# Routed experts with few tokens: two weight passes in place of three, chosen by a branch on TensorE

## The chip, the cores and the metric

One core of a Trainium2 chip runs the whole program in one launch. The metric is the device time of an execution in microseconds (us); less is better. Engines are named as the profile names them: PE (TensorE matmul), PEld (TensorE weight load), DVE (VectorE), ACT (ScalarE), POOL (GpSimd), SP (SyncE, which issues the weight loads).

## What is computed

Two decoder layers over 256 tokens of width 1024: each has a modulated RMSNorm, a mixer of two attention groups, and a feed-forward part (dense in layer 0, experts in layer 1). The change is in the experts of layer 1. Everything is float32.

```python
def moe_swiglu(h, router_w, w_gate, w_up, w_down):
    t = h.reshape(B * S, D)                                   # 256 x 1024
    top_v, top_i = lax.top_k(t @ router_w, 2)
    top_w = jax.nn.softmax(top_v, axis=-1)
    gates = sum of one_hot(top_i, 8) * top_w
    for e in range(8):                                        # w_gate, w_up 1024 x 3584, w_down 3584 x 1024
        y = y + gates[:, e:e + 1] * swiglu(t, w_gate[e], w_up[e], w_down[e])
```

swiglu is (silu(h @ w_gate) * (h @ w_up)) @ w_down. Computing the reference's router on its own inputs gives the tokens of the eight experts: 68, 62, 71, 84, 60, 28, 77 and 62. Experts 1, 4, 5 and 7 have at most 64.

## The kernel before

A float32 product is made of rounded halves: an operand x becomes hi (x in the matmul's float32r format) and lo (x - hi), and a product is the three matmuls hi*hi, hi*lo and lo*hi. So every weight, loaded by SP in units of 128x2048 (1 MiB, tile `raw`, 8 buffers), passes through ACT (`whi`, L160) and DVE (`wlo`, L181). The class `Stream` (`ws`) hands them out in the order of use; it converts as far ahead as its 4 places for `whi` and 3 for `wlo` are free, and SP loads a new unit when DVE is done with an old one.

In `experts` the router picks two experts per token. `pick` makes a 0/1 matrix that gives each token of an expert one of CAP = 128 slots (`pk`; its transposes `back` put results back), `gather` multiplies it with the tokens' hi and lo parts, and ACT copies that to `xe`, for two experts at a time. A branch (`overflow`, L1201) handles experts of more than 128 tokens; here it is passed by.

Then 8 experts x 7 chunks of 512 hidden columns follow. A chunk uses six weight units: two for gate and two for up (`wide`, L1028: 8 values of k, three matmuls of 512 columns each), two for down (`down`, L1071: 4 values of f, six matmuls each). The stationary operand is the 128 slots, hi or lo; the weights move. The order within a chunk is written out by hand: gate of chunk c; in it, after k = 5, `turn` transposes the product of chunk c-1 (L1054) and ACT and DVE split it to `g_hi` (L444) and `g_lo` (L445); silu of gate on ACT (L1149); up of c; down of c-1; and in that, behind f = 1, the product silu * up on DVE (L1167). `finish` (L1084 to L1100: gate row, split, scatter matmul, add to `x_sb`) of an expert is spread over the first two chunks of the next one; `pick` and `gather` of the next two experts stand in the last chunks of experts 1, 3 and 5.

Of the kernel before, what the change touches and what calls it, by code (L numbers as in the profile page):

```python
# [14 lines left out]
F32 = mybir.dt.float32  # L15
# [8 lines left out]
P = 128  # L24
# [9 lines left out]
E = 8  # L34
# [6 lines left out]
FOX_SCALE = 0.125  # L41
NEG = -1.0e30
CAP = P


V_ADAB, V_ATTN, V_FFN, V_QN, V_KVN, V_OUT, V_FB = 0, 48, 56, 64, 66, 67, 75
# [193 lines left out]
def trunk_kernel(ctx: ExitStack, tc: tile.TileContext, x, c, positions, w_early, w_moe, router_w,  # L240
# [656 lines left out]
    def experts(l, outer, ps_x, rs):  # L897
# [8 lines left out]
        posm = outer.tile([P, NB, E], F32, name="posm")  # L906
        gates = outer.tile([P, NB, E], F32, name="gates")
        most = outer.tile([P, 1], I32, name="most")
        w = outer.tile([P, 4, NB], F32, name="w")
        oh = outer.tile([P, 2, NB, E], F32, name="oh")  # L910
        gap(outer, 416)

        def shift_col(k):
            return mod[l][:, 24 + k:25 + k]

        back, xe = {}, {}

        def pick(e):

            pk = outer.tile([P, NB, 2, CAP], F32R, name="pick")  # L920
            for j in range(2):
                for b in range(NB):
                    nc.vector.tensor_scalar(pk[:, b, j], iota, posm[:, b, e + j:e + j + 1], None, ALU.is_equal)
            yield pk
            for j in range(2):
                ps = bank("B", [P, S], "ps_b")
                for b in range(NB):
                    nc.tensor.transpose(ps[:, b * P:(b + 1) * P], pk[:, b, j].bitcast(F32), ident)  # L928
                bt = outer.tile([P, S], F32R if e + j + 1 < E else F32, tag="back", name="back", bufs=3)
                nc.scalar.activation(bt, ps, AF.Copy)  # L930
                back[e + j] = bt
            yield pk

        with tc.tile_pool(name="route", bufs=1, reuse_waits="tile") as pool:
# [48 lines left out]

            nc.vector.scalar_tensor_tensor(posm, ps_p[:, 0:2], 1.0, sel, ALU.add, ALU.mult)
            nc.vector.tensor_scalar(posm, posm, -1.0, None, ALU.add)
            picked = pick(0)
            pk = next(picked)

            def gating():
# [7 lines left out]
                                            w[:, 2 + j, :, None].to_broadcast([P, NB, E]), ALU.mult)  # L997
                nc.vector.tensor_add(gates, of[:, 0], of[:, 1])

            overflow(l, hT, posm, gating, gates, most, [put.args[-1] for put in puts])  # L1000
            ws.pump(1, lazy=True)
            ws.rest(2)

        with tc.tile_pool(name="moe", bufs=1, reuse_waits="tile") as pool:
            def gather(e, pk):

                xe[e], xe[e + 1] = [], []
                for k0 in range(0, KD, 2):
                    for k in range(k0, k0 + 2):
                        both = pool.tile([P, 2, 2, CAP], F32R, name=f"xe{k}")  # L1010
                        ps = bank("B", [P, 2, 2, CAP], "ps_g")
                        for i, part in enumerate((h_hi, h_lo)):
# [3 lines left out]
                        nc.scalar.activation(both, ps, AF.Copy)  # L1016
                        for j in range(2):
                            xe[e + j].append((both[:, 0, j], both[:, 1, j]))
                    yield

            def wide(e, ps):
                for k in range(KD):
                    xe_hi, xe_lo = xe[e][k]
                    c = halves[k % 2]
                    if k % 2 == 0:
                        hi, lo = ws.half()
                    for lh, w in ((xe_hi, hi), (xe_hi, lo), (xe_lo, hi)):
                        nc.tensor.matmul(ps, lh, w[:, c], start=(k == 0 and lh is xe_hi and w is hi),  # L1028
                                         stop=(k == KD - 1 and lh is xe_lo))
                    yield k  # L1030

            y_ps, jobs = {}, deque()

# [6 lines left out]
            def turn(pend):  # L1040
# [2 lines left out]
                yield e, ch, g  # L1043
                if (e, ch) == (E - 1, CH - 1):

                    spare = [pool.tile([P, 2, 2, CAP], F32R, name=f"xe{f}") for f in range(0, NFC, 2)]
                    groups = [(2 * i, 2 * i + 2, [t[:, 0], t[:, 1]]) for i, t in enumerate(spare)]
                else:
                    groups = [(0, NFC, [pool.tile([P, NFC, CAP], F32R, name=f"g_{w}") for w in ("hi", "lo")])]
                for f0, f1, (hi, lo) in groups:  # L1050
                    n = f1 - f0
                    ps = bank("B", [P, n, P], "ps_gt")
                    for i in range(n):
                        nc.tensor.transpose(ps[:, i], act[:, (f0 + i) * P:(f0 + i + 1) * P], ident)  # L1054
                    split(hi[:, :n], lo[:, :n], ps)
                    g += [(hi[:, i], lo[:, i]) for i in range(n)]
                    yield

            def down(pend):
                e, ch, g = pend  # L1060
                if ch == 0:
                    y_ps[e] = [bank("C", [P, 512], "ps_y") for _ in range(2)]
                for f in range(NFC):
                    hi, lo = ws.half()
                    g_hi, g_lo = g[f]
                    last = ch == CH - 1 and f == NFC - 1
                    steps = [(hf, lh, w) for lh, w in ((g_hi, hi), (g_hi, lo), (g_lo, hi)) for hf in range(2)]
                    if last:
                        steps.sort(key=lambda s: s[0])
                    for hf, lh, w in steps:  # L1070
                        nc.tensor.matmul(y_ps[e][hf], lh, w[:, hf * 512:(hf + 1) * 512],  # L1071
                                         start=(ch == 0 and f == 0 and lh is g_hi and w is hi),
                                         stop=(last and lh is g_lo))
                    yield f
                    step()

# [56 lines left out]
            ahead = gather(0, pk)  # L1133
            next(ahead)
            next(ahead)
            next(picked)
            jobs += [None, None, None, None] + puts + [gating]
            for e in range(E):
                for ch in range(CH):
                    pg = bank("A", [P, FC], "ps_gate")  # L1140
                    for k in wide(e, pg):
# [11 lines left out]
                    if (e, ch) == (E - 1, CH - 1):  # L1153
                        nc.scalar.preload_act_table_set("natural_log_exp_and_others")  # L1154
# [337 lines left out]
```

## Time and profile before

| | before |
|---|---|
| median of 3 runs (lowest, highest) | 1524.0 us (1523.59, 1524.49) |
| the profiled execution: its time, span of its instructions | 1524.38 us, 1522.2 us |
| PE busy, PEld busy | 1491.9 us (98%), 1277.0 us (84%) |
| DVE busy, ACT busy | 1265.4 us (83%), 1004.9 us (66%) |
| DMA | 481.73 MB, mean 316 GB/s |
| granted TensorE clock, mean | 0.995 |

Busy time is the union of an engine's instructions. PE is pipelined: a matmul's recorded 0.39 us overlaps the next one's, so the time that one costs is the distance of two starts. The experts run from about 538 us to the end.

### The profile page before, as it was taken

The page shows a single profiled execution, that of the slowest core. Times are in us where ns is not written, and L with a number is a line of the kernel's source. Part 1 is how long each engine was busy: PE and PEld are TensorE (multiplying, and loading weights), DVE is VectorE, ACT ScalarE, POOL GpSimd, SP SyncE. Part 2 cuts the span into 40 slices and gives each one's busy share as a digit, 9 for nine tenths or more (in the row PEclk, how much of TensorE's full clock was granted, in tenths as well). Part 3 has the DMA queues.
Part 4 walks back from the last instruction along what each step waited for, and adds up shares of the span by engine and source line. Part 5 has one row for each costly group of instructions (what it writes and reads, how often), then busy time and mean ns, then how long its engine had stood idle before and what let it go on. Part 6 is the DMA issues. An engine that isn't in the chain of part 4 may idle for free.

```text
span 1522.2 us, 20572 instructions
## 1 busy us (share of the span) xinstructions
PE 1491.9 (98%) x7985; PEld 1277.0 (84%) x7985; DVE 1265.4 (83%) x1209; ACT 1004.9 (66%) x1068; POOL 12.6 (1%) x20
## 2 busy tenths in 40 slices
PE   8999999999999899999999999999999999999997
PEld 7988999999898678888888888888888888888885
DVE  5988877777776678899889889879889888988987
ACT  5575544444657576777677777677777777776774
POOL 1000000000000000000000000000000000000000
PEclk9999999999999999999999999999999999999999
DMA  9974778778581269999999999999999998999992
GB/s 373 412 268 166 290 276 309 287 291 299 186 291 56 84 257 363 378 364 371 366 347 348 373 367 366 371 340 347 377 370 368 373 362 324 369 372 377 360 370 91
DMA packets 68472, 481.73 MB, mean 316 GB/s; under 512 B 7953, under 2 KB 8593, under 8 KB 10770
## 3 DMA queue, kind: packets, MB, share of 16 engines
q1 hardware_dynamic: 68178, 480.33, 83.1%
q8 instruction: 63, 1.03, 0.3%
q14 instruction: 39, 0.32, 0.1%
q0 software_dynamic: 192, 0.05, 0.0%
HBM read 479.25 MB, written 1.05 MB: 316 GB/s over the span
## 4 chain that ended last, share of the span: by engine, by line
PE 63%; DVE 1%; ACT 0%; issue 0%; DVEq 0%; ACTq 0%
PE ps_y L1071 20%; PE ps_gate L1028 20%; PE ps_up L1028 19%; PE ps_gt L1054 2%; PE ps_g L1014 1%; DVE wlo L181 0%; PE ps_sc L1097 0%; PE ps_sc L1098 0%; ACT whi L160 0%; PE ps_sc L1121 0%; PE ps_b L928 0%; DVE fin L1129 0%; ACT L1154 0%; DVE gate L347 0%; ACT junk L399 0%
## 5 line engine op out<-in xcount | busy, mean ns | idle before, releaser
L181 DVE TENSOR_TENSOR wlo<-raw,whi 128x2048 fp32r<-128x2048 f32 (+1 forms) x474 | 923.8, 1975 | 62.5 <-ACT whi L160 57.2
L160 ACT ACTIVATE whi<-raw 128x2048 fp32r<-128x2048 f32 (+1 forms) x474 | 769.9, 1662 | 158.6 <-PE ps_gu L394 77.4
L1028 PE MATMUL ps_gate<-whi,xe 128*128 128x512 f32 x896 | 301.8, 396 | 0.0
L1028 PE MATMUL ps_up<-whi,xe 128*128 128x512 f32 x896 | 288.3, 390 | 0.0
L1028 PEld LDWEIGHTS ps_up<-whi,xe 128*128 128x128 f32 x896 | 168.3, 188 | 35.3
L1028 PEld LDWEIGHTS ps_gate<-whi,xe 128*128 128x128 f32 x896 | 168.3, 188 | 33.4
L1028 PE MATMUL ps_gate<-wlo,xe 128*128 128x512 f32 x448 | 175.1, 391 | 0.7 <-DVE wlo L181 0.7
L1028 PE MATMUL ps_up<-wlo,xe 128*128 128x512 f32 x448 | 174.9, 390 | 0.1
L1071 PE MATMUL ps_y<-wlo,g_hi 128*128 128x512 f32 x440 | 136.8, 389 | 0.4 <-DVE wlo L181 0.4
L1071 PE MATMUL ps_y<-whi,g_hi 128*128 128x512 f32 x440 | 136.7, 389 | 0.0
L1071 PE MATMUL ps_y<-whi,g_lo 128*128 128x512 f32 x440 | 136.6, 389 | 0.0
L393 PE MATMUL ps_gu<-dT_hi,whi 128*128 128x256 f32 x432 | 122.5, 284 | 0.0
L395 PE MATMUL ps_gu<-dT_hi,wlo 128*128 128x256 f32 x432 | 122.2, 283 | 0.0
L394 PE MATMUL ps_gu<-dT_lo,whi 128*128 128x256 f32 x432 | 122.2, 283 | 0.0
L444 ACT ACTIVATE g_hi<-ps_gt 128x512 fp32r<-128x512 f32 x55 | 33.0, 599 | 127.1 <-PE ps_gt L1054 127.1
L1028 PEld LDWEIGHTS ps_up<-wlo,xe 128*128 128x128 f32 x448 | 84.1, 188 | 19.0 <-DVE wlo L181 1.4
L1028 PEld LDWEIGHTS ps_gate<-wlo,xe 128*128 128x128 f32 x448 | 84.3, 188 | 17.0 <-DVE wlo L181 1.3
L1071 PEld LDWEIGHTS ps_y<-wlo,g_hi 128*128 128x128 f32 x440 | 82.4, 188 | 18.0 <-DVE wlo L181 1.0
L445 DVE TENSOR_TENSOR g_lo<-ps_gt,g_hi 128x512 fp32r<-128x512 f32 x55 | 37.9, 689 | 71.4 <-ACT g_hi L444 71.4
L1071 PEld LDWEIGHTS ps_y<-whi,g_lo 128*128 128x128 f32 x440 | 82.6, 188 | 17.2
L1071 PEld LDWEIGHTS ps_y<-whi,g_hi 128*128 128x128 f32 x440 | 82.3, 188 | 16.9
L393 PEld LDWEIGHTS ps_gu<-dT_hi,whi 128*128 128x128 f32 x432 | 82.8, 192 | 1.2 <-issue 0.2
(295 smaller groups left out, 1926.4 us busy)
## 6 DMA issues: line engine op xcount, KB each, us to landing
raw<-in_w_moe_dram SPq DMA_DIRECT2D x336, 1024.0 KB, 6.9
raw<-in_w_early_dram SPq DMA_DIRECT2D x114, 1024.0 KB, 6.8
raw<-in_w_early_dram SPq DMA_DIRECT2D x6, 512.0 KB, 8.6
gate<-in_ada_b_dram SPq DMA_DIRECT2D x4, 512.0 KB, 5.6
x_sb<-in_x_dram SPq DMA_DIRECT2D x1, 1024.0 KB, 7.3
out_dram<-fin SPq DMA_DIRECT2D x4, 256.0 KB, 2.0
fg<-in_final_g_dram SPq DMA_DIRECT2D x1, 512.0 KB, 4.9
cn<-in_consts_dram SPq DMA_DIRECT2D x1, 192.0 KB, 12.6
```

Of the source, the lines that this page charges most:

```text
L160: self.nc.scalar.activation(hi, raw, AF.Copy)
L181: self.nc.vector.tensor_sub(parts[1], raw, parts[0].bitcast(F32))
L393: nc.tensor.matmul(out_, lh, rh, start=start, stop=False)
L394: nc.tensor.matmul(out_, lh, rl, start=False, stop=False)
L395: nc.tensor.matmul(out_, ll, rh, start=False, stop=stop)
L444: nc.scalar.activation(hi, src, AF.Copy)
L445: nc.vector.tensor_sub(lo, src, hi.bitcast(F32))
L1014: nc.tensor.matmul(ps[:, i], part[:, b, k * P:(k + 1) * P], pk[:, b], start=(b == 0), stop=(b == NB - 1))
L1028: nc.tensor.matmul(ps, lh, w[:, c], start=(k == 0 and lh is xe_hi and w is hi), stop=(k == KD - 1 and lh is xe_lo))
L1054: nc.tensor.transpose(ps[:, i], act[:, (f0 + i) * P:(f0 + i + 1) * P], ident)
L1071: nc.tensor.matmul(y_ps[e][hf], lh, w[:, hf * 512:(hf + 1) * 512], start=(ch == 0 and f == 0 and lh is g_hi and w is hi), stop=(last and l ...
```

## The change

The router also computes, per expert, `stretch` (2 where the expert has at most 64 tokens, else 1), and packs a bit per expert into one integer, `bits`, which PE loads into a register once (L1209). `slotm` = position x stretch spreads a small expert's tokens over the even slots. `xe` and `g` now lie as [hi slots, lo slots] in one row, so that `even` (every second element of the 256) is a stationary operand with 64 hi and 64 lo tokens. On PE each half unit (`by_width`, L941) becomes a branch with two bodies: the wide one has the three passes of before, the narrow one two (`even` with hi, `even` with lo), after which rows 0 to 63 and 64 to 127 of the PSUM tile hold two parts of one sum. `folded` adds them for gate and up: ACT copies the tile to `fold`, and in the narrow body one matmul with `onto` adds its lower half to the upper. The copy is made for every expert. For down, the scatter matrix `back` has both rows of a token, so the scatter sums them. silu now stands behind k = 4 of up, the branch of `product` (L1246) is its own where the chunk before belongs to another expert. POOL makes the rows of `back` (four instructions of 128 columns per expert). In `close` of layer 1 one `wlo` is no longer made ahead of the router, and one conversion ahead of the gather is gone.

A diff cut to the core (dots mark what is left out):

```diff
-            rs.append(row_r(ss, D, "x", ws.rest if b else None))
+            rs.append(row_r(ss, D, "x", ws.rest if b and ws.size == SPLIT else None))
...
+        def by_width(e, wide, narrow, *more):
+            with tc.If((held[0] & (1 << e)) == 0) as cmp:
+                wide()
+            with cmp.Else():
+                for steps in (*more, narrow):
+                    steps()
...
+            nc.vector.tensor_scalar(stretch, ps_p[:, 2], NARROW + 0.5, 1.0, ALU.is_lt, ALU.add)
+            nc.vector.tensor_tensor(slotm, posm, stretch[:, None, :].to_broadcast([P, NB, E]), ALU.mult)
...
+            nc.vector.tensor_copy(bits, sums[:, 0:1])
             overflow(l, hT, posm, gating, gates, most, [put.args[-1] for put in puts])
-            ws.pump(1, lazy=True)
...
-            def wide(e, ps):
+            def wide(e, ps, *sums):
                 for k in range(KD):
-                    xe_hi, xe_lo = xe[e][k]
-                    c = halves[k % 2]
                     if k % 2 == 0:
                         hi, lo = ws.half()
-                    for lh, w in ((xe_hi, hi), (xe_hi, lo), (xe_lo, hi)):
-                        nc.tensor.matmul(ps, lh, w[:, c], ...
+                        def products(*passes):
+                            n = 0
+                            for kk in range(k, k + 2):
+                                both = xe[e][kk]
+                                for part, w in passes:
+                                    n += 1
+                                    nc.tensor.matmul(ps, both[:, part], w[:, halves[kk % 2]], ...
+                        first, second, even = slice(0, CAP), slice(CAP, 2 * CAP), slice(0, 2 * CAP, 2)
+                        by_width(e, partial(products, (first, hi), (first, lo), (second, hi)),
+                                 partial(products, (even, hi), (even, lo)), *(sums if k == 4 else ()))
                     yield k
+            def folded(ps):
+                t = pool.tile([P, FC], F32R, name="fold")
+                nc.scalar.activation(t, ps, AF.Copy)
+                return partial(nc.tensor.matmul, ps, onto, t, start=False, stop=True, skip_group_check=True)
...
+                    by_width(e, partial(turns, ident), partial(turns, spread))
...
+                    by_width(e, partial(products, (first, hi), (first, lo), (second, hi)),
+                             partial(products, (even, hi), (even, lo)), *(sums if f == 1 else ()))
...
+            held.append(nc.tensor.value_load(bits[0:1, 0:1], min_val=0, max_val=(1 << E) - 1))
...
+                    add = folded(pg)
                     act = pool.tile([P, FC], F32, name="act")
-                    nc.scalar.activation(act, pg, AF.Silu)
...
-                    for k in wide(e, pu):
+                    for k in wide(e, pu, add):
+                        if k == 4:
+                            nc.scalar.activation(act, pg, AF.Silu)
...
+                    add = folded(pu)
+                    within = pend is not None and pend[0] == e and (e, ch) != (E - 1, CH - 1)
                     def product():
                         if parts:
+                            if not within:
+                                with tc.If((held[0] & (1 << e)) != 0):
+                                    add()
                             c = parts.popleft()
                             nc.vector.tensor_mul(act[:, c], act[:, c], pu[:, c])
...
-                    for f in down(pend) if pend is not None else ():
+                    for f in down(pend, *((add,) if within else ())) if pend is not None else ():
```

How the instructions of two engines stand. First PE, half a unit of up (k = 4 and 5 of one chunk); of before:

```order
L1028 MATMUL ps_up<-whi,xe_6552 128x512
L1028 MATMUL ps_up<-wlo_5012,xe_6552 128x512
L1028 MATMUL ps_up<-whi,xe_6552 128x512
L1028 MATMUL ps_up<-whi,xe_6559 128x512
L1028 MATMUL ps_up<-wlo_5012,xe_6559 128x512
L1028 MATMUL ps_up<-whi,xe_6559 128x512
```

and of the change, where the rows behind the first UNCONDITIONAL_BRANCH are the narrow body:

```order
L941 COMPARE_AND_BRANCH
L1081 MATMUL ps_up<-whi,xe_6607 128x512
L1081 MATMUL ps_up<-wlo,xe_6607 128x512
L1081 MATMUL ps_up<-whi,xe_6607 128x512
L1081 MATMUL ps_up<-whi,xe_6614 128x512
L1081 MATMUL ps_up<-wlo,xe_6614 128x512
L1081 MATMUL ps_up<-whi,xe_6614 128x512
L941 UNCONDITIONAL_BRANCH
L945 MATMUL ps_gate<-fold,onto 128x512
L1081 MATMUL ps_up<-whi,xe_6607 128x512
L1081 MATMUL ps_up<-wlo,xe_6607 128x512
L1081 MATMUL ps_up<-whi,xe_6614 128x512
```

The six matmuls are now one of two bodies behind a compare and a jump, and the narrow body begins with the sum of the gate's two halves. There are 13 such branches in a chunk: four in gate, four in up, one around the transposes, four in down.

Second ACT, one chunk from the split of the turned product on; of before:

```order
L444 ACTIVATE g_hi<-ps_gt 128x512
L1149 ACTIVATE act<-ps_gate 128x512
L160 ACTIVATE whi_5010<-raw_6778 128x2048
L160 ACTIVATE whi_5011<-raw_6806 128x2048
L160 ACTIVATE whi<-raw_6822 128x2048
L160 ACTIVATE whi<-raw_6838 128x2048
L160 ACTIVATE whi_5010<-raw_6855 128x2048
L160 ACTIVATE whi_5011<-raw_6872 128x2048
L444 ACTIVATE g_hi<-ps_gt 128x512
```

and of the change:

```order
L446 ACTIVATE g<-ps_gt 128x4x128
L941 UNCONDITIONAL_BRANCH x3
L1093 ACTIVATE fold<-ps_gate 128x512
L162 ACTIVATE whi_5010<-raw_7001 128x2048
L941 UNCONDITIONAL_BRANCH
L162 ACTIVATE whi_5011<-raw_7050 128x2048
L941 UNCONDITIONAL_BRANCH
L1231 ACTIVATE act<-ps_gate 128x512
L941 UNCONDITIONAL_BRANCH
L1093 ACTIVATE fold<-ps_up 128x512
L162 ACTIVATE whi<-raw_7080 128x2048
L941 UNCONDITIONAL_BRANCH
```

ACT has two more copies in a chunk (`fold`), the silu (`act`) has moved behind two conversions, and each branch of PE is a jump to the next instruction here.

## Rows read from the trace of the kernel before

**Rows 1.** Page, part 1: busy us, share of the span and instructions of each engine.

```profile
PE 1491.9 (98%) x7985; PEld 1277.0 (84%) x7985; DVE 1265.4 (83%) x1209; ACT 1004.9 (66%) x1068; POOL 12.6 (1%) x20
```

**Rows 2.** Chain of waits, 600 to 1500 us: share by line; one long piece.

```profile
by line: PE ps_gate L1028 31.7%; PE ps_y L1071 31.3%; PE ps_up L1028 31.0%; PE ps_gt L1054 2.5%; PE ps_g L1014 1.3%; PE ps_sc L1097 0.7%; PE ps_sc L1098 0.7%; DVE wlo L181 0.3%; ACT whi L160 0.2%; PE ps_b L928 0.1%; ACT L1154 0.1%; issue 0.
...
659.51 5.46 PE ps_up L1028 x24
```

**Rows 3.** Windows: us; busy us (count) PE, PEld, DVE, ACT, POOL; PEclk; DMA share; GB/s.

```profile
701.91:718.70 16.79, 16.79 (x78) 13.89 (x76) 14.59 (x10) 12.26 (x9) 0.00 (x0) 1.00 0.96 375
790.66:809.00 18.34, 18.34 (x84) 15.15 (x83) 17.64 (x15) 14.32 (x11) 0.00 (x0) 1.00 0.87 343
666.39:790.66 124.27, 124.23 (x578) 103.03 (x577) 108.06 (x69) 91.22 (x69) 0.00 (x0) 1.00 0.94 357
790.66:910.20 119.54, 119.54 (x542) 98.87 (x541) 107.12 (x66) 86.92 (x59) 0.00 (x0) 1.00 0.96 367
```

**Rows 4.** Timeline, DVE: start us, us, line, op, tiles, [idle before <- releaser].

```profile
701.91 0.68 DVE L1167 TENSOR_TENSOR act<-act,ps_up 128x512 f32<-128x512 f32 x1
702.50 6.69 DVE L181 TENSOR_TENSOR wlo<-raw,whi 128x2048 fp32r<-128x2048 f32 x3
711.09 0.69 DVE L445 TENSOR_TENSOR g_lo<-ps_gt,g_hi 128x512 fp32r<-128x512 f32 x1 [1.89 <-ACT g_hi L444]
711.70 2.28 DVE L181 TENSOR_TENSOR wlo<-raw,whi 128x2048 fp32r<-128x2048 f32 x1
714.29 4.50 DVE L181 TENSOR_TENSOR wlo<-raw,whi 128x2048 fp32r<-128x2048 f32 x2 [0.31 <-ACT whi L160]
718.70 0.68 DVE L1167 TENSOR_TENSOR act<-act,ps_up 128x512 f32<-128x512 f32 x1
```

**Rows 5.** Waits, 700 to 736 us (two chunks): us in total, times, longest us.

```profile
ACT g_hi L444 <- PE ps_gt L1054: 5.2, 2, 2.6
DVE g_lo L445 <- ACT g_hi L444: 3.8, 2, 1.9
DVE wlo L181 <- ACT whi L160: 0.6, 2, 0.3
```

**Rows 6.** Waits of SyncE's DMA queue, 600 to 1500 us.

```profile
SPq L142 <- DVE wlo L181: 760.5, 306, 5.2
```

**Rows 7.** Windows, for DMA share and GB/s.

```profile
10.00:65.00 55.00, 52.32 (x413) 51.27 (x413) 42.39 (x69) 31.19 (x59) 1.69 (x3) 0.97 1.02 424
565.00:575.00 10.00, 10.00 (x48) 8.29 (x47) 8.10 (x6) 5.97 (x4) 0.00 (x0) 1.00 1.00 415
600.00:700.00 100.00, 100.00 (x454) 82.72 (x453) 89.78 (x55) 71.90 (x50) 0.00 (x0) 1.00 0.97 370
```

**Rows 8.** Waits, 757 to 777 us, where the next two experts are gathered.

```profile
DVE wlo L181 <- ACT whi L160: 6.1, 4, 2.4
```

**Rows 9.** Timeline, PE, before and behind the overflow branch (L1201), and a gather.

```profile
528.56 0.17 PE L977 MATMUL ps_p<-sel,tri 128*128 128x8 bf16 x1
528.58 0.17 PE L978 MATMUL ps_p<-sel,ones 128*128 128x8 bf16 x1
...
533.67 0.77 PE L1014 MATMUL ps_g<-pick,h_hi 128*128 128x256 f32 x2 [4.85 <-ACT whi L160]
...
540.04 0.40 PE L1014 MATMUL ps_g<-pick,h_hi 128*128 128x256 f32 x2
540.28 0.41 PE L1014 MATMUL ps_g<-pick,h_lo 128*128 128x256 f32 x2
```

**Rows 10.** Timeline, ACT, two conversions with the overflow branch between them.

```profile
529.61 3.94 ACT L160 ACTIVATE whi<-raw 128x2048 fp32r<-128x2048 f32 x2
```

**Rows 11.** Timeline, PEld: a weight load behind idle time with no wait.

```profile
527.03 0.19 PEld L351 LDWEIGHTS ps_fold<-acc,cn 128*128 128x128 f32 x1 [0.24 <-issue]
```

**Rows 12.** Page, part 3: the larger of two instruction queues: packets, MB.

```profile
q8 instruction: 63, 1.03, 0.3%
```

More of the change, by code (lines that the diff above doesn't have):

```diff
@@ L43 @@
 CAP = P
+NARROW = 64
 V_ADAB, V_ATTN, V_FFN, V_QN, V_KVN, V_OUT, V_FB = 0, 48, 56, 64, 66, 67, 75
@@ L908, in experts @@
         most = outer.tile([P, 1], I32, name="most")
+        bits = outer.tile([P, 1], I32, name="bits")
+        powers = outer.tile([P, E], F32, name="powers")
+        for e in range(E):
+            nc.gpsimd.memset(powers[:, e:e + 1], float(1 << e))
+        stretch = outer.tile([P, E], F32, name="stretch")
+        slotm = outer.tile([P, NB, E], F32, name="slotm")
         w = outer.tile([P, 4, NB], F32, name="w")
         oh = outer.tile([P, 2, NB, E], F32, name="oh")
-        gap(outer, 416)
+        gap(outer, 256)
+        less = outer.tile([P, CAP], F32, name="less")
+        base = outer.tile([P, CAP], F32, name="base")
+        onto = outer.tile([P, P], F32R, name="onto")
+        spread = outer.tile([P, P], F32, name="spread")
+        for i in range(2):
+            nc.gpsimd.tensor_copy(spread[:, i::2], ident[:, i * NARROW:(i + 1) * NARROW])
+        nc.gpsimd.tensor_scalar(less, iota, NARROW - 0.5, -float(NARROW), ALU.is_gt, ALU.mult)
+        nc.gpsimd.tensor_sub(base, iota, less)
+        nc.gpsimd.tensor_scalar(onto[:, NARROW:], ident[:, NARROW:], 0.0, None, ALU.mult)
+        nc.gpsimd.tensor_copy(onto[:, :NARROW], ident[:, NARROW:])
         def shift_col(k):
             return mod[l][:, 24 + k:25 + k]
+        def by_width(e, wide, narrow, *more):
[4 more added lines that the diff above has]
+                    steps()
+        held = []
         back, xe = {}, {}
@@ L922, in pick @@
                 for b in range(NB):
-                    nc.vector.tensor_scalar(pk[:, b, j], iota, posm[:, b, e + j:e + j + 1], None, ALU.is_equal)
+                    nc.vector.tensor_scalar(pk[:, b, j], iota, slotm[:, b, e + j:e + j + 1], None, ALU.is_equal)
             yield pk
+            rows_of = []
+            for j in range(2):
+                slot = outer.tile([P, CAP], F32, name="slot")
+                nc.gpsimd.tensor_scalar(slot, less, stretch[:, e + j:e + j + 1], None, ALU.mult)
+                nc.gpsimd.tensor_add(slot, slot, base)
+                pb = outer.tile([P, NB, CAP], F32, name="pickb", bufs=2)
+                for b in range(NB):
+                    nc.gpsimd.tensor_scalar(pb[:, b], slot, posm[:, b, e + j:e + j + 1], None, ALU.is_equal)
+                rows_of.append(pb)
             for j in range(2):
@@ L927, in pick @@
                 for b in range(NB):
-                    nc.tensor.transpose(ps[:, b * P:(b + 1) * P], pk[:, b, j].bitcast(F32), ident)
+                    nc.tensor.transpose(ps[:, b * P:(b + 1) * P], rows_of[j][:, b], ident)
                 bt = outer.tile([P, S], F32R if e + j + 1 < E else F32, tag="back", name="back", bufs=3)
@@ L998, in gating @@
                 nc.vector.tensor_add(gates, of[:, 0], of[:, 1])
+            sums = scratch([P, E + 1], F32, "bitsum")
+            nc.vector.tensor_tensor_reduce(out=sums[:, 1:], in0=stretch, in1=powers, scale=1.0, scalar=1.0 - (1 << E),
+                                           op0=ALU.mult, op1=ALU.add, accum_out=sums[:, 0:1])
+            nc.vector.tensor_copy(bits, sums[:, 0:1])
             overflow(l, hT, posm, gating, gates, most, [put.args[-1] for put in puts])
-            ws.pump(1, lazy=True)
             ws.rest(2)
@@ L1015, in gather @@
                                                  start=(b == 0), stop=(b == NB - 1))
-                        nc.scalar.activation(both, ps, AF.Copy)
+                        nc.scalar.activation(both, ps.rearrange("p w j s -> p j w s"), AF.Copy)
                         for j in range(2):
-                            xe[e + j].append((both[:, 0, j], both[:, 1, j]))
+                            xe[e + j].append(both[:, j].rearrange("p w s -> p (w s)"))
                     yield
-            def wide(e, ps):
+            def wide(e, ps, *sums):
                 for k in range(KD):
-                    xe_hi, xe_lo = xe[e][k]
-                    c = halves[k % 2]
                     if k % 2 == 0:
                         hi, lo = ws.half()
-                    for lh, w in ((xe_hi, hi), (xe_hi, lo), (xe_lo, hi)):
-                        nc.tensor.matmul(ps, lh, w[:, c], start=(k == 0 and lh is xe_hi and w is hi),
-                                         stop=(k == KD - 1 and lh is xe_lo))
+                        def products(*passes):
[4 more added lines that the diff above has]
+                                    n += 1
+                                    nc.tensor.matmul(ps, both[:, part], w[:, halves[kk % 2]], start=(k == 0 and n == 1),
+                                                     stop=(k == KD - 2 and n == 2 * len(passes)))
+                        first, second, even = slice(0, CAP), slice(CAP, 2 * CAP), slice(0, 2 * CAP, 2)
+                        by_width(e, partial(products, (first, hi), (first, lo), (second, hi)),
+                                 partial(products, (even, hi), (even, lo)), *(sums if k == 4 else ()))
                     yield k
+            def folded(ps):
+                t = pool.tile([P, FC], F32R, name="fold")
+                nc.scalar.activation(t, ps, AF.Copy)
+                return partial(nc.tensor.matmul, ps, onto, t, start=False, stop=True, skip_group_check=True)
             y_ps, jobs = {}, deque()
@@ L1044, in turn, with turns, down @@
                 if (e, ch) == (E - 1, CH - 1):
-                    spare = [pool.tile([P, 2, 2, CAP], F32R, name=f"xe{f}") for f in range(0, NFC, 2)]
-                    groups = [(2 * i, 2 * i + 2, [t[:, 0], t[:, 1]]) for i, t in enumerate(spare)]
-                else:
-                    groups = [(0, NFC, [pool.tile([P, NFC, CAP], F32R, name=f"g_{w}") for w in ("hi", "lo")])]
-                for f0, f1, (hi, lo) in groups:
+                    groups = [(f, f + 2, pool.tile([P, 2, 2, CAP], F32R, name=f"xe{f}")) for f in range(0, NFC, 2)]
+                else:
+                    groups = [(0, NFC, pool.tile([P, NFC, 2, CAP], F32R, name="g"))]
+                for f0, f1, both in groups:
                     n = f1 - f0
                     ps = bank("B", [P, n, P], "ps_gt")
[L1053 to L1056, printed above, removed]
+                    def turns(order):
+                        for i in range(n):
+                            nc.tensor.transpose(ps[:, i], act[:, (f0 + i) * P:(f0 + i + 1) * P], order)
+                    by_width(e, partial(turns, ident), partial(turns, spread))
+                    split(both[:, :n, 0], both[:, :n, 1], ps)
+                    g += [both[:, i].rearrange("p w s -> p (w s)") for i in range(n)]
                     yield
-            def down(pend):
+            def down(pend, *sums):
                 e, ch, g = pend
@@ L1064, in down, with products @@
                     hi, lo = ws.half()
[L1065 to L1073, printed above, removed]
+                    both = g[f]
+                    def products(*passes):
+                        first, last = ch == 0 and f == 0, ch == CH - 1 and f == NFC - 1
+                        steps = [(n, hf) for n in range(len(passes)) for hf in range(2)]
+                        if last:
+                            steps.sort(key=lambda s: s[1])
+                        for n, hf in steps:
+                            part, w = passes[n]
+                            nc.tensor.matmul(y_ps[e][hf], both[:, part], w[:, halves[hf]], start=(first and n == 0),
+                                             stop=(last and n == len(passes) - 1))
+                    first, second, even = slice(0, CAP), slice(CAP, 2 * CAP), slice(0, 2 * CAP, 2)
+                    by_width(e, partial(products, (first, hi), (first, lo), (second, hi)),
+                             partial(products, (even, hi), (even, lo)), *(sums if f == 1 else ()))
                     yield f
```

4 lines of the change are left out of this document (2 added, 2 removed).

## The prediction

> **What bounds the kernel now.** I read the page first [rows 1]: PE is busy 98% of the span, but DVE has 83% and the weight loads run beside both, so PE's share alone says little. The chain of waits in the experts' stretch [rows 2] decides: 94% of it are the matmuls of gate, up and down, and DVE and ACT together have half a per cent. One piece gives the price of a matmul: 24 in 5.46 us, 0.2275 us each, whatever its operands. A regular chunk takes 16.79 us from one product on DVE to the next [rows 3]: 72 such matmuls are 16.4, the transposes the rest.
>
> The next views say what stands behind PE. In that chunk DVE is busy 14.59 us and ACT 12.26 [rows 3]. The timeline of DVE [rows 4] has one long gap in it, 1.89 us ahead of the split of the turned product, and the waits [rows 5] show its source: ACT waits for PE's transposes, DVE for ACT. So most of DVE's idle time is PE's lateness, handed on. SP's queue waits for DVE's `wlo` in 760 of 900 us [rows 6]: it has no free buffer, so loaded units stand ready. DMA, though, is not far from its own limit: 370 GB/s here, against 424 and 415 in the two stretches where it was fed without a break [rows 7].
>
> **The change, part by part.** The sum is made against the profiled execution, 1524.38 us, 0.4 above the median of the runs and inside their spread.
>
> *Narrow chunks, PE.* Experts 1, 4, 5 and 7 have at most 64 tokens, so 28 of 56 chunks take the short bodies. Each drops 24 matmuls and adds two sums: 22 x 0.2275 = 5.0 us less, 11.8 left. PE stops being the bound there.
>
> *Narrow chunks, DVE.* Its work does not change: six `wlo` 2.20 us apart ((6.69 - 2.28) / 2), a split of 0.61 and a product of 0.60 [rows 4], back to back. Does it still wait? Between the `wlo` of gate's second unit and the split stands one other `wlo`, 2.20 us. In that time PE needs four matmuls (0.91) and the transposes (0.4), ACT a copy (0.6): 1.9, so the gap of 1.89 closes. The product now waits longer: from the `wlo` of up's second unit on PE makes nine matmuls (2.05), ACT the copy `fold` (0.6), PE half a down unit and a sum (1.14), 3.8 in all; DVE has two `wlo`, 4.4, in between. That closes too, with 0.6 to spare. What stays are DVE's waits for `whi`, 0.31 a chunk (0.6 in two chunks, [rows 5]). If ACT had no time for its two further copies, this is where it would show: 12.26 + 1.2 = 13.5 of 14.6, so it has. I take DVE's busy time of a whole expert [rows 3] plus 7 x 0.31: an even one 107.1 + 2.2 = 109.3 for 119.5, 10.2 less. An odd one also gathers for the next two, where DVE waited 6.1 us for ACT, which waited behind PE's gather [rows 8]; I keep half, between nothing and all of it, since ACT's eight copies stay and PE's queue in front of them shrinks: 108.1 + 2.2 + 2.9 = 113.2 for 124.3, 11.1 less. The last expert ends the program, so it has six of seven such steps: 8.7. Together 2 x 11.1 + 10.2 + 8.7 = 41.1 us less.
>
> *The tail.* Behind the last product stand one and a half chunks of down: 12 matmuls fewer, 2.7; I take 2.0, since the last `wlo` may be late.
>
> *Wide chunks, branches.* The other 28 chunks keep all 72 matmuls and get 13 branches each, 364. The trace of before has no branch in a stream of matmuls. From below the cost is nothing: the five small matmuls behind a wait start 0.02 us apart [rows 9], so they stood ready while the first one waited, and PE is fed ahead of time; and ACT runs two conversions in 3.94 us with the overflow branch between them, no gap [rows 10]. A gain is excluded: a branch does no work that was done before. From above, the shortest idle time that waited for nothing shown is 0.24 us [rows 11]: 364 x 0.24 = 87 us. I take nothing, because a body of six matmuls lasts 1.4 us and the rows on a stream that is fed ahead are the nearer ones; 87 stays for the range.
>
> [...]
>
> *Wide chunks, order on ACT.* silu moves behind two conversions and the product waits for half a down unit more. By the same count as above DVE gets every unit converted before PE needs it, but with less room. I take 0.2 us a chunk, 5.6; ends are 0 and one copy of 0.6 each, 17.
>
> *Router and start.* Four small operations on DVE and one register load on PE are added to a path from which a `wlo` of 2.28 us goes: nothing, 2 us either way. POOL's rows run beside the first gather.
>
> *Weight loads with stride two.* Before has none. In the gather two matmuls with their loads take 0.24 us [rows 9], the last two,, so a load takes 0.12 at most; twice that is 0.24, against 0.2275 that a matmul covers: 48 x 0.012 = 0.6 us a narrow chunk on an engine with 2.8 to spare. Nothing.
>
> Sum: 1524.4 - 41.1 - 2.0 + 5.6 = **1487 us**.
>
> **The rivals.**
>
> *PE waits at the branches (slower).* The place is the wide chunk, where PE has no slack: what a branch exposes is paid in full, 364 times, while narrow chunks hide it behind DVE. It decides from (41.1 + 2.0 - 5.6) / 364 = 0.10 us a branch; at 0.24 the time is 1487 + 87 = 1574. For it: compare, jump and a wait within a body are new, and behind the overflow branch PE was silent for 4.85 us [rows 9]. Against it: that gap was put down to a conversion on ACT, and the branch passed over a large body. Its second form is code that is late: one queue brought 63 packets of 16 KB [rows 12], which fits PE's 2 x 7985 instructions [rows 1], 253 a packet; a wide chunk now steps through about 300 with its unused bodies, so some 34 packets fall in wide chunks, and 34 waits of up to 4.85 us would be 165 us, 1652 at the worst. [...]
>
> *DMA becomes the bound.* A chunk needs 6.29 MB; at 14.9 us that is 422 GB/s, as much as the best stretch. If the rate of the experts' stretch cannot rise beyond 370 / 0.97 = 381 GB/s [rows 7], a narrow chunk takes 16.5 us, an expert 115.6: 2 x 8.7 + 3.9 + 3.3 + 2.0 less, 5.6 more, 1503 us. For it: a share of 0.97 at 370. Against it: 415 at 570 us with all engines at work, and loaded units in store at the start of a narrow expert.
>
> *The hand-overs take the place of PE.* If fold, sum and product form a chain that DVE cannot cover, a narrow chunk stays at 16.8 and nothing is left but 5.6 of cost: 1522 to 1530. My count has 0.6 us of room for it, so this is unlikely.
>
> *The branch is not taken.* Two experts have 62 tokens; three tokens routed otherwise would be needed. I give it nothing.
>
> **How the numbers follow.** Forecast 0.62, DMA 0.13, hand-overs 0.06, branches 0.19. A measurement of this kernel tells about 0.2%, 3 us, from no change. Faster: forecast, DMA and the few branch cases under 0.10 us, 0.77; same 0.04; slower 0.19. Low end: no waits at all in narrow experts (12.4 + 2 x 16.2 + 10.6 less), a full tail and no cost in the wide ones, 1466; I take 1468. High end: the branch case up to two thirds of its upper price of 0.24, 0.16 us each, 1487 + 58 = 1545; beyond lie about 0.09. The likeliest case alone spans 1468 to 1505.
>
> **What would show it.** Right: regular narrow chunks of 14.6 to 15.2 us between products, DVE without its gap ahead of the split, no PE idle time within wide chunks, which stay at 16.8 to 17.1, and DMA near 420 GB/s in narrow experts. Wrong: matmuls of a wide chunk that start over 0.25 us apart at body borders; ACT waiting for loads; DVE waiting for PE ahead of the product.

## The result, and the profile after

The changed kernel takes 1479.87 us (median of 4, 1479.41 to 1480.85) against 1524.03 in the same session: ratio 0.9711, 95% interval 0.9694 to 0.9728, 44.2 us less. The forecast was 1487, 37 less.

Page, part 1, of the changed kernel, beside [rows 1]:

```profile
PE 1394.8 (94%) x7369; PEld 1157.9 (78%) x7369; DVE 1265.6 (86%) x1214; ACT 1051.5 (71%) x1180; POOL 54.9 (4%) x66
```

PE has 616 matmuls fewer and is busy 97 us less, DVE is busy as long as before, ACT 47 us more. The chain of waits by line, first in expert 7 (small, 1365 to 1457 us), then in expert 6 (large, 1266 to 1350), beside [rows 2]:

```profile
by line: DVE wlo L183 46.2%; issue 23.5%; PE ps_gate L1081 8.3%; ACT whi L162 4.0%; DVE x_sb L1173 3.1%; PE ps_up L1081 2.1%; PE ps_gt L1119 1.9%; PE ps_y L1141 1.8%; DVE act L1249 1.7%; ACT L1233 1.4%; DVE yt L1157 1.3%; DVEq L183 1.0%; AC
...
by line: PE ps_gate L1081 32.6%; PE ps_up L1081 32.4%; PE ps_y L1141 31.6%; PE ps_gt L1119 2.6%; PE ps_sc L1171 0.5%; PE ps_sc L1170 0.5%
```

Large experts still hang on PE, small ones now on DVE's `wlo`. The 23.5% called issue have no releaser in this view; one of the longest pieces of it, 1409.92 to 1412.00 us, lies within three `wlo` that DVE makes without a break (1407.60 to 1414.28). Windows, with the columns of [rows 3]: a wide chunk, two narrow ones, all of expert 4, all of expert 5, and the chunk in which large expert 3 follows large expert 2:

```profile
601.59:618.38 16.79, 16.79 (x78) 13.90 (x77) 14.69 (x8) 13.10 (x11) 0.00 (x0) 1.00 0.99 383
1103.78:1118.21 14.43, 13.12 (x56) 9.57 (x54) 14.43 (x10) 13.00 (x11) 0.00 (x0) 1.00 1.01 426
1118.21:1132.63 14.42, 13.13 (x56) 9.73 (x54) 14.42 (x9) 12.96 (x11) 0.00 (x0) 1.00 1.01 426
1025.82:1132.63 106.81, 95.26 (x392) 69.46 (x390) 106.11 (x64) 91.26 (x72) 0.00 (x0) 1.00 1.00 401
1132.63:1246.60 113.97, 101.11 (x436) 75.35 (x434) 107.39 (x70) 96.76 (x83) 0.00 (x0) 1.00 0.99 402
884.52:902.30 17.78, 17.59 (x80) 14.22 (x78) 14.67 (x8) 14.07 (x12) 0.00 (x0) 1.00 0.93 364
```

The wide chunk, with its 13 branches, lasts what it lasted in [rows 3]. In a narrow chunk DVE is busy from end to end (14.43 of 14.43 us). Its timeline there has none of the gaps of [rows 4]:

```profile
1103.76 0.68 DVE L1249 TENSOR_TENSOR act<-act,ps_up 128x512 f32<-128x512 f32 x1
1104.36 6.69 DVE L183 TENSOR_TENSOR wlo<-raw,whi 128x2048 fp32r<-128x2048 f32 x3
1110.98 0.69 DVE L447 TENSOR_TENSOR g<-ps_gt,g 128x512 fp32r<-128x512 f32 x1
1111.59 6.69 DVE L183 TENSOR_TENSOR wlo<-raw,whi 128x2048 fp32r<-128x2048 f32 x3
```

Where the 43.1 us between the two spans went, from product to product:

| stretch | forecast | measured |
|---|---|---|
| small experts 1, 4, 5, 7 | -41.1 | -10.3, -12.7, -10.4, -9.2: -42.5 |
| large experts 0, 2, 3, 6 | +5.6 | -0.8, +1.4, -0.7, -0.9: -1.1 |
| up to the first product | 0 | +1.9 (552.5 to 554.4) |
| behind the last product | -2.0 | -1.5 (22.7 to 21.2) |

The period of a large expert ends with the first product of the next one; where that is small, gate and up of this last step are narrow already, 1.3, 2.6 and 1.3 us less in experts 0, 3 and 6. Without those the large experts cost 4.1 more.

### The profile page after: what moved, and what is told of

It reads as the page before. It is cut to its first block, busy times and chain, and to the rows that moved or that the text cites. A ratio compares the mean times of both kernels' runs of the same rounds, so it can differ in the third digit from the quotient of the medians.

```text
span 1479.1 us, 21469 instructions
## 1 busy us (share of the span) xinstructions
PE 1394.8 (94%) x7369; PEld 1157.9 (78%) x7369; DVE 1265.6 (86%) x1214; ACT 1051.5 (71%) x1180; POOL 54.9 (4%) x66
## 5 line engine op out<-in xcount | busy, mean ns | idle before, releaser
L1081 PE MATMUL ps_gate<-whi,xe 128*128 128x512 f32 x672 | 242.8, 401 | 0.4 <-PEq L1246 0.4
L1081 PE MATMUL ps_up<-whi,xe 128*128 128x512 f32 x672 | 232.2, 391 | 0.0
L1141 PE MATMUL ps_y<-whi,g 128*128 128x512 f32 x664 | 194.6, 392 | 1.6 <-PEq L1246 1.5
L1141 PEld LDWEIGHTS ps_y<-whi,g 128*128 128x128 f32 x664 | 125.2, 190 | 28.1 <-issue 2.8
L1081 PEld LDWEIGHTS ps_up<-whi,xe 128*128 128x128 f32 x672 | 127.8, 190 | 24.6 <-issue 0.2
L1141 PE MATMUL ps_y<-wlo,g 128*128 128x512 f32 x440 | 142.2, 402 | 2.3 <-DVE wlo L183 2.3
L1141 PEld LDWEIGHTS ps_y<-wlo,g 128*128 128x128 f32 x440 | 80.3, 191 | 28.3 <-DVE wlo L183 14.8
L396 PEld LDWEIGHTS ps_gu<-dT_lo,whi 128*128 128x128 f32 x432 | 82.8, 192 | 1.2 <-issue 0.2
L397 PEld LDWEIGHTS ps_gu<-dT_hi,wlo 128*128 128x128 f32 x432 | 82.8, 192 | 0.0
L330 DVE CUSTOM_DVE_ANT_0 raw<-raw,c_row,vc 128x1024 f32<-128x1024 f32 x56 | 71.1, 1278 | 0.0
```

Source lines behind the costliest of these rows:

```text
L330: nc.vector.tensor_tensor_reduce(out=w, in0=w, in1=c_row, scale=1.0, scalar=vec(l, V_ADAB + section * KD + k, 1), op0=ALU.mult, op1=ALU.ad ...
L396: nc.tensor.matmul(out_, lh, rl, start=False, stop=False)
L397: nc.tensor.matmul(out_, ll, rh, start=False, stop=stop)
L1081: nc.tensor.matmul(ps, both[:, part], w[:, halves[kk % 2]], start=(k == 0 and n == 1), stop=(k == KD - 2 and n == 2 * len(passes)))
L1141: nc.tensor.matmul(y_ps[e][hf], both[:, part], w[:, halves[hf]], start=(first and n == 0), stop=(last and n == len(passes) - 1))
```

## The experiments

**What the branches cost.** Two kernels in which every expert counts as large; the second has no branch.

```diff
-            nc.vector.tensor_scalar(stretch, ps_p[:, 2], NARROW + 0.5, 1.0, ALU.is_lt, ALU.add)
+            nc.vector.tensor_scalar(stretch, ps_p[:, 2], -1.0, 1.0, ALU.is_lt, ALU.add)
```

> The changed kernel, but the threshold of 64 tokens is set so that no expert counts as small: every branch is executed and all 56 chunks take the wide body. Theory (a branch between bodies of six matmuls costs PE nothing; what costs is the product's own branch at a border of two experts, 17.81 us for 16.79 in the one wide-to-wide border of the changed kernel's trace, 7 x 1.0; the start, 1.9; 0.33 in the third chunk of an expert, 7 times; 1.4 at each of three gathers): 1524.0 + 7 + 1.9 + 2.3 + 4.2 = 1539 us, regular chunks at 16.8. Rival (each of the 738 branches is paid where PE has no slack, 0.10 us or more): 1598 us or more, regular chunks at 18.1 or more.

> As all_wide, but the bodies stand there without branches, the copies to fold, the new order on ACT and the router's additions stay. Theory: only the borders' 7 us go, 1532 us. Rival (branches are paid everywhere): some 60 us or more under all_wide, at about 1532 with all_wide at 1598.

all_wide took 1535.8 us (ratio 1.0075, 1.0058 to 1.0092), no_branch 1528.2 (1.0031, 1.0020 to 1.0043). The medians are 7.6 apart, the two profiled spans 9.8 (1535.3 and 1525.5). Regular chunks last 16.8 in both. Of the 9.8, 5.8 are the seven borders, the steps from one expert into the next: 17.8 each in all_wide, in no_branch 16.8, or 17.2 behind a gather. 2.9 lie ahead of the first product, where the clock came back at different times (see The start below), and 1.1 in the rest. At a border the product waits in all_wide, and not in no_branch (DVE's timeline of each):

```profile
917.07 0.69 DVE L1249 TENSOR_TENSOR act<-act,ps_up 128x512 f32<-128x512 f32 x1 [1.35 <-PEq L1246]
```

```profile
910.74 0.68 DVE L1242 TENSOR_TENSOR act<-act,ps_up 128x512 f32<-128x512 f32 x1
```

What no_branch has over before, 4.2 by the medians and 3.2 by the profiled spans, is the price of the copies and the new order: 0.4 to 0.5 in each of six experts, 0.1 in the first and 0.9 in the last, not 0.2 in each chunk.

**How short a body may be.** all_wide with a branch per three matmuls, and per matmul:

```diff
-                        by_width(e, partial(products, (first, hi), (first, lo), (second, hi)),
-                                 partial(products, (even, hi), (even, lo)), *(sums if k == 4 else ()))
+                        for kk in range(k, k + 2):
+                            for i in range(0, 3, BODY):
+                                by_width(e, partial(products, kk, i, 3, *three[i:i + BODY]),
...
```

> As all_wide, but each matmul has a branch of its own: 73 branches a chunk in place of 13, bodies of 0.23 us in place of 1.4. Theory (PE's queue is filled ahead of the array, and a branch is hidden as long as it takes less than its body): within 5 us of all_wide if a branch takes less than 0.23 us, otherwise the excess times 56 x 72. Rival (a fixed price for each, hidden or not, 0.10 us): 56 x 60 x 0.10 = 336 us over all_wide.

> As all_wide and bodies_of_1, now with three matmuls to a branch: about 25 branches a chunk, bodies of 3 x 0.2275 = 0.68 us. In bodies_of_1 a branch with its one matmul came every 0.48 us. Theory (the branch runs ahead of the array, a body costs whichever is longer, its matmuls or the 0.48 us of the branch): 0.68 is longer, so within 5 us of all_wide, 1536 us. Rival (each branch beyond 13 a chunk costs its 0.25 us, 0.48 - 0.2275): 56 x 12 x 0.25 = 168 us over all_wide, 1704 us.

Bodies of three took 1537.3, 1.5 above all_wide, bodies of one 2561.8, 1026 above it. A chunk of each (windows, columns of [rows 3]), and the weight loads' waits in the second's (us in total, times, longest):

```profile
585.00:601.80 16.80, 16.80 (x78) 13.92 (x77) 14.77 (x9) 13.11 (x11) 0.00 (x0) 1.00 0.98 355
```

```profile
877.70:913.40 35.70, 34.84 (x77) 13.96 (x77) 14.88 (x9) 13.43 (x11) 0.00 (x0) 1.00 0.47 178
```

```profile
PEld ps_y L1144 <- issue: 7.6, 25, 0.4
PEld ps_up L1079 <- issue: 7.2, 24, 0.4
PEld ps_gate L1079 <- issue: 7.0, 23, 0.6
```

PE's queue also has the branches themselves on record (their count, and the least, median and longest duration in ns). First the same chunk of bodies of one, then that of bodies of three:

```profile
L942 PEldq COMPARE_BRANCH  x147: 66/169/288, 877.8 to 913.3; - x147
L942 PEldq ALU_OP  x73: 36/36/36, 878.0 to 913.1; - x73
```

```profile
L942 PEldq COMPARE_BRANCH  x51: 66/169/288, 584.9 to 601.7; - x51
```

Each branch is an AND on the register (0.036 us), a compare ahead of the body (0.066) and a jump behind it (0.169 to 0.288). They last as long in either kernel. Matmuls with a branch each start about 0.48 us apart and wait for nothing but their issue; with bodies of three, 0.68 us of matmuls, the chunk is no longer than without branches. So in these runs a branch cost nothing where its body was 0.68 us of matmuls or more; where it was one matmul of 0.2275, PE's queue took 0.48 for branch and body, and that set the pace. Bodies of two matmuls were not tried. A fixed price for each branch falls: it is nothing at three matmuls (1.5 us for 672 branches more), and about 0.25 (0.48 - 0.2275) at one, which for 56 x 72 matmuls makes some 1020 of the 1026 us. My two bounds, 0 and 0.24, are both there, and the length of the body decides between them.

**What bounds a narrow chunk.** First all experts small (threshold 300; the tokens behind the 64th of four experts are left out).

> The changed kernel with the threshold at 300: all experts take the narrow bodies, so the tokens behind the 64th of experts 0, 2, 3 and 6 are left out of the sum. Theory (a narrow chunk lasts as long as DVE's work, 14.4 us, and stays there however many follow each other): experts 0 100.1, odd ones 3 x 114.0, even ones 3 x 106.8, the last 92.8, with 554.4 ahead and 21.2 behind: span 1431, time about 1432. Rival (the loads cannot be sustained at 436 GB/s, the share of 1.01 at 426 in the trace is their end, and the mean over a narrow expert, 403, is what they can hold): 352.3 MB at 403 are 874 us in place of 855, time about 1451, and the narrow chunks get slower towards the end.

all_narrow took 1424.9 us, nearer the theory's time. Odd experts lasted 112.0, even ones 106.8, and regular chunks 14.42 to 14.46 to the end: no loss to the loads, at 413 GB/s over the 107 us from 1049 to 1156.

Then DVE's work was cut in two ways: POOL makes half of one `wlo` a chunk (pool1; two halves in pool2), or nobody does (half_less; four halves in four_less).

```diff
-            self.nc.vector.tensor_sub(parts[1], raw, parts[0].bitcast(F32))
+        cut = n - SPLIT if n == RAW and (i - self.first + 2) % 6 in (1,) else n
+        self.nc.vector.tensor_sub(lo[:, :cut], raw[:, :cut], hi[:, :cut])
+        if cut < n:
+            self.nc.gpsimd.tensor_sub(lo[:, cut:], raw[:, cut:], hi[:, cut:])
```

> The changed kernel, but of the second weight unit of each gate the second half of wlo is made by POOL in place of DVE, which then has 1.0 us less in each chunk (a half of 2.2, less a new instruction's start). Theory (DVE's sum is the bound of a narrow chunk, loaded units stand in store): a regular narrow chunk of 14.42 goes to 13.4; over a whole narrow expert the loads then set the end, 44.0 MB at 426 GB/s, 103.4 us: expert 4 3.4 us less, experts 1 and 5 7 each, expert 7 4, in all 21 less, 1459 us. Rival one (DMA, at a share of 1.01 in these chunks, is the bound already): regular narrow chunks stay at 14.4, less than 8 us in all. Rival two (POOL and DVE get in each other's way, so that DVE's own instructions get longer by what POOL does): narrow chunks longer than 14.4, 1480 or more.

> As pool1, with two halves in a chunk (gate's second unit and down's first). Theory: DVE's sum would allow 12.4, but loads at 426 GB/s need 14.77 a chunk once the store is used up, so no more than 3 us under pool1, and SP's queue no longer waits for DVE in narrow experts. Rival one: as pool1. Rival two: worse than pool1 by as much again.

pool1 took 1530.8, 51 more than the change (37.5 of them in the small experts, 9.0 in the large ones, 4.7 ahead of the first product), and pool2 1586.7, as much again. DVE and POOL in a narrow chunk of pool1:

```profile
1101.32 7.83 DVE L192 TENSOR_TENSOR wlo<-raw,whi 128x2048 fp32r<-128x2048 f32 x3
...
1102.68 3.18 POOL L194 TENSOR_TENSOR wlo<-raw,whi 128x1024 fp32r<-128x1024 f32 x1 [9.97 <-ACT whi L163]
```

The three `wlo`, one of them now a half, take 7.83 us; without POOL the same three take 5.62 (below). Beside POOL's 3.18 us DVE loses 2.2, twice the 1.07 that POOL takes over, and the chunk is 15.6. Rival two holds. Why DVE's instructions get longer beside POOL's is not shown.

> The changed kernel, but from the thirteenth unit on the second half of wlo of each gate's second unit is not made at all (PE multiplies with what an earlier unit left there): DVE has 1.0 us less in each chunk, as in pool1, and POOL does nothing. Theory (DVE's sum is the bound of a narrow chunk): a regular narrow chunk of 14.42 goes to 13.4 while loaded units are in store, and towards 14.77 a chunk (6.29 MB at 426 GB/s) only where they run out; experts 1 and 5 7 us less each, 4 between 3.4 and 7, 7 some 6: 1453 to 1457 us; wide chunks as they were. Rival (DMA is the bound of a narrow chunk already): regular narrow chunks stay at 14.4, the whole gains less than 8 us, 1472 or more.

> As half_less with four halves left out (both units of gate, the second of up, the first of down): DVE 10.4 us a chunk. Theory (the next bound is DMA): a narrow expert of 44.0 MB at 426 GB/s lasts 103.4 us, so experts 1 and 5 10.5 less each, 4 3.4, 7 some 4: about 1452 us, hardly under half_less, SP's queue waits little for DVE and DVE and ACT wait for loads. Rival (the next bound is ACT, 13.0 us a chunk): regular narrow chunks at 13.0 to 13.4, expert 4 at 97 to 99, about 1440 us.

half_less took 1464.6, 15 less than the change and between the theory's time and the rival's. DVE's timeline in a narrow chunk of it:

```profile
1082.58 5.62 DVE L192 TENSOR_TENSOR wlo<-raw,whi 128x2048 fp32r<-128x2048 f32 x3
1088.87 0.69 DVE L455 TENSOR_TENSOR g<-ps_gt,g 128x512 fp32r<-128x512 f32 x1 [0.67 <-ACT g L454]
1089.48 6.69 DVE L192 TENSOR_TENSOR wlo<-raw,whi 128x2048 fp32r<-128x2048 f32 x3
```

Of the 1.07 us taken from DVE 0.67 come back as a wait for the turned product, and the chunk goes from 14.42 to 14.10. So DVE's sum was the bound, but the hand-over from PE by ACT stood right behind it. four_less took 1435.3, lower than either theory. A window of expert 4 and one of expert 5, and ACT's waits from 1104 to 1180 us:

```profile
1036.10:1049.00 12.90, 12.63 (x56) 9.97 (x55) 10.62 (x10) 12.90 (x11) 0.00 (x0) 1.00 1.02 427
...
1149.40:1164.10 14.70, 12.94 (x56) 9.84 (x55) 10.65 (x10) 13.27 (x11) 0.00 (x0) 1.00 1.01 425
```

```profile
ACT whi L163 <- DMA raw<-in_w_moe_dram: 5.3, 11, 0.8
```

At first ACT is busy throughout (12.9 of 12.9), the rival's chunk; at the end of expert 4 the loaded units run out, and expert 5 goes at 14.6 to 15.1, with ACT waiting for loads: 6.29 MB at 425 GB/s are 14.8. Both bounds are there, one behind the other: the theory had left out that units loaded ahead, in the wide experts before, carry a small expert for a while.

**The start.** In the change PE waits 0.83 us for POOL's rows ahead of the first gate. late_rows takes these transposes out of the way:

```diff
-            next(picked)
-            jobs += [None, None, None, None] + puts + [gating]
+            jobs += [None, None, None, None] + puts + [gating, partial(next, picked)]
```

> The changed kernel, with the transposes of POOL's rows for the first two experts put behind the first jobs of expert 0, so that PE doesn't wait 0.83 us for POOL ahead of the first gate. Theory (the first product comes 1.9 us later than before since PE's pause kept the granted clock at 0.5 until 541.9 us in place of 538): the clock rises earlier, about 2 us less, 1478 us. Rival (it is later because one conversion is no longer made ahead of the gather): within 0.8 us of 1479.9.

1479.8, no change. Windows at 540 to 542 us of before, of the change, of late_rows, and of four_less and half_less, whose start has the change's own code (they leave out `wlo` from the thirteenth unit on). The clock stands third from the end:

```profile
540.00:542.00 2.00, 2.00 (x14) 1.77 (x14) 0.00 (x0) 1.09 (x2) 0.00 (x0) 1.00 0.81 340
```

```profile
540.00:542.00 2.00, 2.00 (x7) 1.57 (x6) 0.20 (x1) 1.77 (x1) 1.81 (x4) 0.55 0.93 393
```

```profile
540.00:542.00 2.00, 2.00 (x14) 1.82 (x13) 1.04 (x1) 1.86 (x3) 1.19 (x3) 1.00 0.97 410
```

```profile
540.00:542.00 2.00, 2.00 (x14) 1.83 (x13) 0.94 (x1) 2.00 (x3) 1.91 (x3) 1.00 0.27 111
```

```profile
540.00:542.00 2.00, 2.00 (x9) 1.71 (x8) 1.10 (x1) 0.86 (x1) 1.82 (x4) 0.50 0.44 184
```

In the change the granted clock was 0.55 over these 2 us (0.50 from 534 to 541, 1.00 from 542 on), after waits of 4.70 us ahead of the gather and of 0.83 for POOL; before was at 1.00 by then. In late_rows the clock is back, and the first product comes at 553.5 in place of 554.4; the time of the whole kernel shows nothing of it. But the wait for POOL does not decide it: with the change's own start the clock was back in four_less, whose first product came at 552.6, and not in half_less, where it came at 554.8. no_branch waited 0.89 us for POOL's rows too, stood at 1.00 in this stretch and had its product at 552.2. So the first product follows the clock (552.2 to 553.5 where it stood at 1.00 in this stretch, 554.4 and 554.8 where it stood at 0.55 and 0.50), and the 1.9 us are no fixed cost of the change. The time of late_rows is the rival's, but its reason is not shown: four_less makes that conversion no earlier either. What sets the moment at which the clock comes back stays open.

**The border.** The sum of up's halves without a branch, with a matrix of zeros for large experts, and, since no_border slowed the wide chunks down, the change with an unused gap 32 bytes larger:

```diff
-                                with tc.If((held[0] & (1 << e)) != 0):
-                                    add()
+                                add()
```

> The changed kernel without the branch around the sum of up's halves where two experts meet and at the end: the matmul is always made, with a matrix that POOL makes per expert, onto for a small one and zeros for a large one. Theory (in that branch the wide arm makes PE wait until its own matmuls are done before the product is released, 0.41 us of PE and 1.0 of the chunk): the chunk from expert 2 to 3 goes from 17.81 to 16.8, the three other places where a large expert begins gain up to 1.0 each: 1476 to 1479 us. Rival (the border's 1.0 us comes from the later finish or from ACT): no change, 1479.9 within 0.7.

```diff
-        gap(outer, 256)
+        gap(outer, 288)
```

> The changed kernel with one number changed: an unused gap of 256 bytes per partition becomes 288, so that everything behind it (xe and g, PE's stationary operands, among them) lies 32 bytes further on, as in no_border. Theory (in no_border matmuls of large experts came 0.2335 us apart in place of 0.2275, because the stationary operands no longer begin at a multiple of 64 bytes): wide chunks go from 16.80 to 17.2, 72 x 0.006, 26 of them, narrow ones stay: 1490 us. Rival (the matrices that POOL made, or the code that had moved, slowed no_border down): 1479.9 within 0.7.

no_border took 1491.5, shift32 1491.0: the whole loss comes with the 32 bytes. 24 matmuls of a large expert in the chain of waits, of shift32 and of the change:

```profile
1284.08 5.60 PE ps_up L1081 x24
```

```profile
1275.05 5.44 PE ps_up L1081 x24
```

Each takes 0.2333 us for 0.2267, so wide chunks take 17.23; narrow ones stay at 14.43, with PE not their bound. Compared with shift32, no_border gains nothing, and its step from expert 2 to 3 is as long (18.32 and 18.26). no_border's theory falls: it is not the branch's wide arm. DVE's waits of no_border, 890 to 910 us:

```profile
DVE act L1254 <- PE ps_up L1252: 1.6, 1, 1.6
```

L1252 is the sum. The product waits for its matmul as it waited for the branch in the change (1.35 us at this border): either stands behind the 12 matmuls of down's first unit in PE's queue.

## Why the prediction was right, point by point

- *Narrow chunks on DVE:* right, and the reason of the gain. The count of the gaps that close held; what I had left in, 0.31 us a chunk for `whi`, is gone as well, so a regular chunk is 14.42, under the 14.6 to 15.2 I gave, and expert 4 gained 12.7 for 10.2: of the 2.5, 1.5 are idle time of DVE (0.7 for the 2.2 I had left in), the rest is busy time (106.1 for 107.1). That is the term that was mis-sized. In odd experts 10.3 and 10.4 were gained for 11.1. DVE's waits in expert 5:

```profile
DVE wlo L183 <- ACT whi L162: 2.7, 3, 1.9
DVE act L1249 <- PE ps_up L945: 1.8, 1, 1.8
DVE g L447 <- ACT g L446: 0.9, 1, 0.9
DVE y_lo L1165 <- ACT y_hi L1161: 0.7, 1, 0.7
DVE act L1249 <- PEq L1246: 0.5, 1, 0.5
```

All its waits for `whi` came to 2.7, 1.9 of them at the gather; I had allowed 5.1, 2.9 of them there. What I had not counted are the product's wait for the sum behind the gather (1.8), the waits of the last step, in which expert 6 is wide already (0.9 and 0.5), and the 0.7 of the finish. So DVE is idle for 6.6 us of 114.0.

- *Tail:* 1.5 for 2.0, a little less than I took.
- *Branches at nothing:* right for bodies of six, in 28 chunks and, in all_wide, in 56. The row that I held to be the nearer one was. The rival's second form, late code, came with 33 packets more than in [rows 12] (page, part 3) and cost nothing that a wide chunk shows:

```profile
q8 instruction: 96, 1.57, 0.4%
```

- *Order on ACT, +5.6:* the sum was near (4.1), its place was wrong. Regular wide chunks pay nothing; the first step of expert 0 pays 0.5, the third chunk of each large expert but the first 0.4, the gather in expert 3 1.5, and the border from expert 2 to 3 1.0. The last is a wait that I had not counted: the product behind its own branch.
- *Router and start at nothing, within 2 either way:* +1.9 in the profiled execution, at the end of what I had allowed. It follows the clock, which came back at other times in other executions of the same start.
- *A step between a large and a small expert* is half narrow. I had given all seven steps to the expert they start in. That put 5.1 us of gain into the large experts' line, and took 4 from the small ones' (the last steps of experts 1 and 5 last 16.9 and 17.0, in all_narrow 15.0). So the small experts' 42.5 for 41.1 is nearer than its parts: narrow chunks were faster than forecast, and these two steps hid most of it.
- *Rivals.* DMA as a bound at 381 GB/s fell: narrow chunks ran at 426, as the 420 I had asked for, and all_narrow held 413. It is a bound, at 425, but only once DVE has less to do and the store is used up (four_less). The hand-overs did not decide, but half_less met one after 0.32 us: not the product, to which I had given 0.6 of room, but the split, for which my count had left 0.3 (2.20 against 1.9). Branches had a cost only with one matmul in a body (0.25 us each), not with three or six.

None of the variants that compute the whole result beat the change; late_rows equals it.

## What to carry to other kernels

In these runs a branch on PE was free where its body was three matmuls of 512 columns or more, and cost 0.25 us where it was one: put the branch around half a unit of work, not around a matmul. When one engine loses a third of its work, read from the timeline how long every other engine needs for the same piece, with its hand-overs; the next bound is the largest, and here three more (14.1, 12.9, and the loads' 14.8 as soon as nothing is left in store) lay within 2 us. A helper engine may cost the first one more than it takes over: here POOL took 1.07 us from DVE and cost it 2.2.

## What the runs showed that I had not expected

- Moving PE's stationary operands and the tiles beside them by 32 bytes made the matmuls 2.9% slower, 0.2333 us for 0.2267, at a granted clock of 1.00: 11 us of the kernel. Which of the moved tiles does it, and whether other distances do, was not tried; so that a multiple of 64 bytes decides is not shown.
- A branch around every matmul doubled a chunk, 35.7 us for 16.8, 0.48 us a matmul, with no wait in the trace but the issue. The branch's own records are as long where it costs nothing.
- POOL's subtraction of 128x1024 takes 3.18 us beside DVE and lengthens DVE's by 2.2.
